# A hybrid decoder layer on one core: the w_ada tiles loaded in one lot, block 2's u summed over six accumulators, the SSM tables queued behind h

## The chip, the core and the metric

The kernel runs on one core of a Trainium2 chip. Its metric is the device time of one execution in microseconds, median of the runs shown. The engines have queues of their own and run side by side: TensorE (PE, with weight loads as PEld), VectorE (DVE), ScalarE (ACT), GpSimd (POOL) and SyncE (SP), which issues nearly all DMAs here.

## The reference, cut to what matters

One decoder layer over 2048 tokens of width 1024. The part in question is the start of the layer:

```python
silu_c = jax.nn.silu(c)
mod = (silu_c @ w_ada[l] + b_ada[l])[:, None, :]
sh_m, sc_m, gt_m, sh_f, sc_f, gt_f = jnp.split(mod, N_MOD, axis=-1)
h = rmsnorm(x, g_mix[l]) * (1.0 + sc_m) + sh_m
proj = h @ w_in[l]
q, k, v, f_logit, u = jnp.split(proj, [...], axis=-1)
...
attn = rmsnorm(forgetting_attention(q, k, v, log_f), g_attn_out[l])
ssm = rmsnorm(s5_ssm(u, a_re[l], a_im[l], log_dt[l], ...), g_ssm_out[l])
mix = jnp.concatenate([attn, ssm], axis=-1) @ w_out[l]
x = x + gt_m * mix
# then a gated MLP with a causal convolution, and a final rmsnorm
```

Nothing of h can be computed before `sh_m` and `sc_m`, the first two sections of silu(c) @ w_ada; and the SSM needs tables that follow from a, dt, B and C alone (powers of exp(lambda dt), sines and cosines).

## The kernel before

Tokens are taken in four blocks of 512 (`TB`), channels in eight tiles of 128 (`KT`), channels on the partitions. All matrix products of the layer are made of three matmuls, hi x hi, hi x lo and lo x hi, of operands split into an fp32r part and its rest: a `w_raw` tile from memory gives `w_hi` on ACT (L86) and `w_lo` on VectorE (L87); a channel tile of h is made by `modulate` as `h_f` (VectorE, L402), `h_hi` (ACT, L390) and `h_lo` (VectorE, L391). There are two `h_f` buffers, and for blocks 2 and 3 each `h_f` is also stored to memory (`f_d`) by SP.

The begin runs like this. `load_x(2)` loads block 2's x and its squares (`sq_acc`, L344), whose sums give the factor `rt` through TensorE, VectorE (`rs_y`), TensorE's transposes (L358) and a copy on ACT (L378). `load_u_weights` loads two weight slots for u. `ada_first` computes the first two sections of the modulation in two halves of 512 channels: 16 tiles `wada` of 256 KB for each half, those of the shift summed by TensorE (L296), those of the scale by VectorE (L298, L300), in 18 buffers that h will use later. The second half's sums end in `mod_gm` and `mod_sm` (L329, L310) of channel tiles 4 to 7. `ssm_tables` then sets up the tables: nine small loads, a chain of some 230 VectorE operations, most of them 128x16, and a function `batches` that makes four batches of larger ones (128x512, 128x576), each with matmuls on TensorE (L787, L788, L802) and stores; batch q may issue after a matmul `marks[q]`.

`proj_u(b)` makes h of a block and projects u and the forget logits: columns in two halves (`cc` 2, 264 wide, and `cc` 3, 256 wide), tokens in four groups `s` of 128. For block 2, half 2 runs k-outer over four accumulators `proj_ps`, so that each channel tile of h is used as it comes; all else is one accumulator after another. An accumulator is copied out by ACT (`f_all` L456, `ust` L458, two buffers) and stored by SP. The order is u of blocks 2, 3, 1, then `proj_qkv(1)`, u of block 0, `proj_qkv(0)`, with three more sections of the modulation (`ada_late`, L319 and L321, w_ada tiles of 512 KB) on VectorE beside them. Attention, SSM, output projection and the MLP follow and are most of the span.

The order in which instructions stand in each engine's queue is set by a scheduler from the program's order, its own estimates, and constraints such as `tc.issue_after(ins)`, which places what is in its block behind the instruction given. Each engine's queue is then worked off strictly in that order.

## Time and profile before

| | |
|---|---|
| median of 3 runs (lowest, highest) | 2625.82 us (2625.49, 2627.09) |
| span of the profiled execution, first to last instruction | 2625.8 us |
| PE, DVE, ACT, POOL busy | 97%, 78%, 48%, 6% |
| mean DMA rate | 197 GB/s |
| span up to block 2's u done / block 1's u done | 83 us / 165 us |

The profiled execution is the one that the page shows; its span agrees with the median, and nothing worth naming lies around it. In the rows of a timeline stand the start and length in us, engine, line, operation, output and inputs; "x4" is a count, and what stands in brackets at the end is the engine's idle time before and what ended it. A bar is longer than the step from one instruction to the next where engines overlap the two.

### The profile page before, as it was taken

What the parts mean: (1) busy time and instruction counts of PE and PEld (TensorE: products, weight loads), DVE (VectorE), ACT (ScalarE), POOL (GpSimd) and SP (SyncE); (2) the same over time, 40 slices, a digit from 0 to 9 for tenths busy, and PEclk for the clock granted to TensorE, in tenths of its full rate; (3) what the DMA queues carried; (4) which work ended last, traced back from release to release, by engine and by line L of the source; (5) the groups of instructions that cost most, each with busy time, mean ns of one, the idle gap of its engine ahead of it and who ended that gap; (6) DMA issues with size and microseconds to landing.
All of it is one profiled execution on the core that took longest, in us unless ns stands there. A gap on an engine that the chain in (4) does not pass through costs nothing.

```text
span 2625.8 us, 35861 instructions
## 1 busy us (share of the span) xinstructions
PE 2539.7 (97%) x12235; PEld 2056.0 (78%) x12235; DVE 2043.4 (78%) x3824; ACT 1257.6 (48%) x2120; POOL 145.9 (6%) x130
## 2 busy tenths in 40 slices
PE   6999999998999999999999999999989999999997
PEld 3888877887788787888778888888767888887776
DVE  7989688966887878787877777776589888876777
ACT  3423255644454545455545555556554555543213
POOL 0001000000000000000000000000002333320000
PEclk8899999998999999999999999999999999999998
DMA  9476986667556655556557555556733443447573
GB/s 318 150 250 217 299 263 199 198 190 236 173 190 215 199 184 184 191 178 207 176 196 224 184 171 192 170 182 225 245 103 128 168 153 136 153 144 289 190 277 119
DMA packets 269319, 516.37 MB, mean 197 GB/s; under 512 B 27952, under 2 KB 114864, under 8 KB 269136
## 3 DMA queue, kind: packets, MB, share of 16 engines
q1 hardware_dynamic: 267312, 508.84, 58.4%
q0 software_dynamic: 1280, 4.20, 0.4%
q8 instruction: 97, 1.59, 0.3%
q10 hardware_dynamic: 544, 1.05, 0.1%
q14 instruction: 86, 0.70, 0.1%
HBM read 374.32 MB, written 139.59 MB: 196 GB/s over the span
## 4 chain that ended last, share of the span: by engine, by line
PE 80%; DMA 7%; DVE 7%; issue 2%; ACT 2%; SPq 1%; POOL 0%; DVEq 0%; POOLq 0%; ACTq 0%
PE ff_ps L1258 19%; PE up_x L1382 7%; PE ff_ps L1232 7%; PE up_z L1382 5%; PE up_y L1382 4%; PE ff_ps L1290 3%; PE ff_ps L1292 3%; PE ff_ps L1291 3%; PE o_ps L1018 2%; PE o_ps L1022 2%; DMA wada<-in_w_ada 2%; PE proj_ps L439 2%; PE acc_x L1612 2%; PE vq_ps L472 2%; PE qs_ps L472 2%
## 5 line engine op out<-in xcount | busy, mean ns | idle before, releaser
L86 ACT CAST w_hi<-w_raw 128x1024 fp32r<-128x1024 f32 (+4 forms) x187 | 173.1, 927 | 270.5 <-DMA w_raw<-in_w_flat 71.6
L1258 PE MATMUL ff_ps<-h_lo,w_hi 128*128 128x512 f32 x704 | 279.8, 397 | 0.8 <-DVE h_lo L391 0.8
L1258 PE MATMUL ff_ps<-h_hi,w_lo 128*128 128x512 f32 x704 | 280.0, 398 | 0.0
L1258 PE MATMUL ff_ps<-h_hi,w_hi 128*128 128x512 f32 x704 | 279.8, 399 | 0.0
L87 DVE TENSOR_TENSOR w_lo<-w_raw,w_hi 128x1024 fp32r<-128x1024 f32 (+4 forms) x187 | 199.8, 1069 | 64.4 <-ACT w_hi L86 52.5
L1009 DVE TENSOR_TENSOR pl<-pf,ph 128x512 fp32r<-128x512 f32 (+1 forms) x320 | 194.9, 618 | 19.8 <-ACT ph L1008 17.1
L1008 ACT CAST ph<-pf 128x512 fp32r<-128x512 f32 (+1 forms) x320 | 177.9, 569 | 62.4 <-PE o_ps L1018 56.4
L1017 DVE TENSOR_TENSOR acc<-acc,pf 128x512 f32<-128x512 f32 (+2 forms) x264 | 159.2, 605 | 26.0 <-ACT pf L1007 23.5
L1007 ACT ACTIVATE pf<-sc_ps 128x512 f32<-128x512 f32 (+2 forms) x184 | 98.3, 539 | 123.3 <-PE sc_ps L998 74.7
L1258 PEld LDWEIGHTS ff_ps<-h_lo,w_hi 128*128 128x128 f32 x704 | 133.6, 190 | 29.5 <-DVE h_lo L391 1.1
L1258 PEld LDWEIGHTS ff_ps<-h_hi,w_lo 128*128 128x128 f32 x704 | 133.5, 190 | 28.8
L1258 PEld LDWEIGHTS ff_ps<-h_hi,w_hi 128*128 128x128 f32 x704 | 133.4, 190 | 28.6 <-issue 0.2
L116 ACT CAST w_hi<-w_raw 128x1024 fp32r<-128x1024 f32 (+2 forms) x100 | 96.4, 964 | 103.7 <-PE ff_ps L1232 41.9
L1291 PE MATMUL ff_ps<-act_lo,w_hi 128*128 128x512 f32 x352 | 139.6, 397 | 0.0
L1290 PE MATMUL ff_ps<-act_hi,w_hi 128*128 128x512 f32 x352 | 139.4, 398 | 0.2 <-ACT rt L378 0.2
L1292 PE MATMUL ff_ps<-act_hi,w_lo 128*128 128x512 f32 x352 | 139.4, 397 | 0.0
L959 DVE TENSOR_REDUCE mx<-sc_ps 128x1 f32<-128x512 f32 (+2 forms) x164 | 97.6, 599 | 52.4 <-PE sc_ps L958 25.9
L1018 PE MATMUL o_ps<-ph,vv 128*128 128x512 f32 (+1 forms) x320 | 121.2, 380 | 2.2 <-ACT ph L1008 2.2
L1022 PE MATMUL o_ps<-pl,vv 128*128 128x512 f32 (+2 forms) x312 | 116.2, 375 | 0.9 <-DVE pl L1009 0.9
L1382 PE MATMUL up_x<-hh,w_hi 128*128 128x512 f32 x352 | 112.7, 400 | 3.4 <-ACT hh L387 1.8
L1364 POOL TENSOR_TENSOR s<-v_raw 128x512 f32<-128x512 f32 x18 | 27.7, 1538 | 1518.9 <-DVE w_lo L87 1518.9
L86 ACT CAST w_hi<-s 128x1024 fp32r<-128x1024 f32 (+2 forms) x66 | 62.1, 944 | 81.8 <-DVE s L1583 31.7
(678 smaller groups left out, 6961.1 us busy)
## 6 DMA issues: line engine op xcount, KB each, us to landing
w_raw<-in_w_flat SPq DMA_DIRECT2D x193, 512.0 KB
w_lo<-wlo SPq DMA_DIRECT2D x68, 512.0 KB
wlo<-w_lo SPq DMA_DIRECT2D x52, 512.0 KB
kb<-kb SPq DMA_DIRECT2D x80, 256.0 KB
vv<-v SPq DMA_DIRECT2D x80, 256.0 KB
w_raw<-in_w_flat SPq DMA_DIRECT2D x40, 384.0 KB
w_raw<-in_w_flat SPq DMA_DIRECT2D x40, 320.0 KB
wada<-in_w_ada SPq DMA_DIRECT2D x48, 256.0 KB
```

The lines of the kernel that those rows point to most:

```text
L86: nc.scalar.copy(hi[:, :n], raw[:, :n])
L87: nc.vector.tensor_tensor(out=lo[:, :n], in0=raw[:, :n], in1=hi[:, :n].bitcast(F32), op=ALU.subtract)
L1008: A.copy(ph[:, cs], pf[:, cs])
L1009: V.tensor_tensor(out=pl[:, cs], in0=pf[:, cs], in1=ph[:, cs].bitcast(F32), op=ALU.subtract)
L1018: T.matmul(o_ps[:, cs], lhsT=vt[:, i, :], rhs=ph[:, cs], start=first, stop=False)
L1022: T.matmul(o_ps[:, cs], lhsT=vt[:, i, :], rhs=pl[:, cs], start=False, stop=(b > 0 and ch == b - 1 and i == 3))
L1232: mark[0] = T.matmul(ps, lhsT=lt, rhs=rt, start=(i == 0), stop=(i == 23))
L1258: T.matmul(ps, lhsT=lt, rhs=rt, start=(n == 0), stop=(n == 23))
L1290: T.matmul(ps, lhsT=a, rhs=ah[:, ts], start=(c == 0), stop=False)
L1291: T.matmul(ps, lhsT=a, rhs=al[:, ts], start=False, stop=False)
L1292: mark[0] = T.matmul(ps, lhsT=bb, rhs=ah[:, ts], start=False, stop=(c == n - 1))
L1382: mark[0] = T.matmul(ps, lhsT=lt, rhs=rt, start=(first and n == 0), stop=(n == 11), skip_group_check=not first)
```

## The change

- `ada_first` has 32 places for its tiles: the 18 h buffers, six `vq` tiles and eight halves of `w_hi`, `w_lo` tiles. No load waits for a tile to come free. The two sums on TensorE share one PSUM tile, in partitions 0 and 32, which leaves the `qs` bank free. The second pair of u weight slots is loaded between the two halves.
- Block 2's u runs k-outer over six accumulators: the four of half 2 and two of half 3, both in the `qs` bank. Two are left for after.
- `ssm_tables` is called after block 2's u and stands behind block 2's last `h_lo`; `proj_qkv(1)` stands behind block 1's last `h_lo`; the four batches stand behind u of block 3, u of block 1, and the first two q tiles of block 1, instead of u of blocks 2, 3, 1 and 1.

```diff
-    def ada_first():
-
-        ps_fns = (vq_ps, lambda: qs_psum.tile([P, TB], F32, name="ada_ps", tag="qs", bufs=1))
+    def ada_first(between):
+
+        places = [hp.tile([P, TB], F32, name="wada", tag=t, bufs=9) for _ in range(9) for t in ("h_hi", "h_lo")]
+        places += [f("wada", [P, TB + 2 * (f is vq_a)], F32)[:, 0:TB] for _ in range(2) for f in (vq_a, vq_b, vq_c)]
+        for tag in ("w_hi", "w_lo"):
+            for _ in range(2):
+                t = wpool.tile([P, 1024], F32, name="wada", tag=tag, bufs=3)
+                places += [t[:, 0:TB], t[:, TB : 2 * TB]]
+        both = vq_ps()
         for hf in range(2):
+            if hf:
+                between()
             cols, js = slice(hf * TB, (hf + 1) * TB), slice(hf * 4, hf * 4 + 4)
             acc = ap_.tile([P, D], F32, name="ada_acc", tag="ada_acc", bufs=2)[:, 0:TB]
-            ps = ps_fns[hf]()
+            ps = both[32 * hf : 32 * hf + 1, :]
             for k in range(KT):
-                wt = [hp.tile([P, TB], F32, name="wada", tag=t, bufs=9) for t in ("h_hi", "h_lo")]
+                wt = [places.pop(0) for _ in range(2)]
                 for sec in range(2):
                     Q.dma_start(wt[sec], w_ada[sec, k, :, cols])
...
+    split_last = [None]
...
-            V.scalar_tensor_tensor(out=lo, in0=f, scalar=shift, in1=hi.bitcast(F32), op0=ALU.add, op1=ALU.subtract)
+            split_last[0] = V.scalar_tensor_tensor(out=lo, in0=f, scalar=shift, in1=hi.bitcast(F32), op0=ALU.add,
+                                                   op1=ALU.subtract)
...
-    def token_rows(pss, h, s0, sl, n):
+    def token_rows(jobs, h):
 
         for k in range(KT):
             hi, lo = h[k]
-            wh, wl = sl[k // 4]
-            c0 = (k % 4) * n
-            for i, ps in enumerate(pss):
-                ts = slice((s0 + i) * P, (s0 + i + 1) * P)
-                lh, ll = hi[:, ts], lo[:, ts]
+            for ps, i, sl, n, first in jobs:
+                wh, wl = (t[:, (k % 4) * n : (k % 4 + 1) * n] for t in sl[k // 4])
+                lh, ll = (t[:, i * P : (i + 1) * P] for t in (hi, lo))
...
     def proj_u(b, rows, wu):
         h = modulate(*rows, mod["gm"], mod["sm"], f_d.get(b))
+        sl = {cc: wu[(cc - 2) * 2 : (cc - 2) * 2 + 2] for cc in (2, 3)}
+        width = {cc: vfu_slots[cc * 2][2] for cc in (2, 3)}
+        done = {}
+        if b == 2:
+            bank = qs_psum.tile([P, TB], F32, name="u_ps", tag="qs", bufs=1)
+            done = {(2, s): (proj_ps(), True) for s in range(4)}
+            done.update({(3, s): (bank[:, s * 256 : (s + 1) * 256], s == 0) for s in range(2)})
+            token_rows([(ps, s, sl[cc], width[cc], first) for (cc, s), (ps, first) in done.items()], h)
         for cc in (2, 3):
-            n = vfu_slots[cc * 2][2]
-            sl = wu[(cc - 2) * 2 : (cc - 2) * 2 + 2]
-            pss = [proj_ps() for _ in range(4)] if (b, cc) in ((2, 2),) else [None] * 4
-            if pss[0] is not None:
-                token_rows(pss, h, 0, sl, n)
-            for s, ps in enumerate(pss):
-                if ps is None:
+            for s in range(4):
+                if (cc, s) in done:
+                    ps = done[cc, s][0]
+                else:
                     ps = proj_ps()
-                    token_rows([ps], h, s, sl, n)
+                    token_rows([(ps, s, sl[cc], width[cc], True)], h)
...
-        ada_first()
-        batches = ssm_tables(pp)
-        wu += load_u_weights(wup, vfu_slots[6:8])
+        ada_first(lambda: wu.extend(load_u_weights(wup, vfu_slots[6:8])))
         marks = []
         for b in (2, 3, 1):
             h = proj_u(b, rows0 if b == 2 else load_x(b), wu)
             marks.append(mark[0])
-        batches(marks + marks[-1:])
+            if b == 2:
+                with tc.issue_after(split_last[0].ins):
+                    batches = ssm_tables(pp)
         rows0 = load_x(0)
-        proj_qkv(1, h, pair_ps(qs_psum))
+        with tc.issue_after(split_last[0].ins):
+            proj_qkv(1, h, pair_ps(qs_psum), marks=marks)
+        batches(marks[1:5])
```

Three places show what the scheduler makes of it. The first is VectorE while block 2's h is made. Before, between the third and fourth of its channel tiles (`ex_`, `sc_` are steps of the tables' chain):

```order
L87 TENSOR_TENSOR w_lo<-w_raw,w_hi 128x1024
L402 SCALAR_TENSOR_TENSOR h_f<-xt,mod_gm,rt 128x512
L87 TENSOR_TENSOR w_lo<-w_raw,w_hi 128x1024
L615 TENSOR_SCALAR sc_sp<-sc_sp 128x16
L620 TENSOR_SCALAR sc_cp<-sc_cp 128x16
L524 TENSOR_SCALAR ex_p<-ex_p 128x16
L402 SCALAR_TENSOR_TENSOR h_f<-xt,mod_gm,rt 128x512
L344 TENSOR_TENSOR sq_acc<-sq_acc,sq 128x512
L614 TENSOR_TENSOR sc_sp<-sc_sp,sc_r_554 128x16
L619 TENSOR_TENSOR sc_cp<-sc_cp,sc_r_554 128x16
L523 TENSOR_TENSOR ex_p<-ex_p,ex_r 128x16
L391 SCALAR_TENSOR_TENSOR h_lo<-h_f,mod_sm,h_hi 128x512
```

Squares, splits and the chain's steps stand between the pieces of h. The same place now, from the second half's `mod_sm` on:

```order
L318 TENSOR_TENSOR mod_sm<-prep_ps,bcol 128x4
L352 TENSOR_TENSOR sq_acc<-sq_acc,sq 128x512 x2
L413 SCALAR_TENSOR_TENSOR h_f<-xt,mod_gm,rt 128x512
L352 TENSOR_TENSOR sq_acc<-sq_acc,sq 128x512
L413 SCALAR_TENSOR_TENSOR h_f<-xt,mod_gm,rt 128x512
L401 SCALAR_TENSOR_TENSOR h_lo<-h_f,mod_sm,h_hi 128x512
L352 TENSOR_TENSOR sq_acc<-sq_acc,sq 128x512 x2
L401 SCALAR_TENSOR_TENSOR h_lo<-h_f,mod_sm,h_hi 128x512
L413 SCALAR_TENSOR_TENSOR h_f<-xt,mod_gm,rt 128x512 x2
L401 SCALAR_TENSOR_TENSOR h_lo<-h_f,mod_sm,h_hi 128x512 x2
```

Only h and the squares of block 3's x are left there; the splits `w_lo` and the chain stand further back. The second place is VectorE behind block 2's last `h_lo`, now:

```order
L401 SCALAR_TENSOR_TENSOR h_lo<-h_f,mod_sm,h_hi 128x512 x2
L675 TENSOR_SCALAR hb<-hb 128x32
L530 TENSOR_SCALAR ex_x<-tb_ld 128x16
L695 MEMSET tb_lr 128x16
L696 MEMSET tb_li 128x16
L712 TENSOR_TENSOR tb_den<-tb_ar 128x16
L713 TENSOR_TENSOR tb_t_891<-tb_ai 128x16
L352 TENSOR_TENSOR sq_acc<-sq_acc,sq 128x512
L531 TENSOR_SCALAR ex_n<-ex_x 128x16
```

There the chain begins, some 100 of its operations ahead of block 3's first `h_f`; before, some 180 stood ahead of that `h_f`, a good half of them ahead of block 2's last `h_lo`. The third place is TensorE at one channel tile of block 2's u, with the buffers' numbers. Before, the tile 882 (`h_hi`) and 883 (`h_lo`) goes through four accumulators, 928 to 931:

```order
L439 MATMUL proj_ps_928<-wu_hi_316,h_hi_882 128x264
L439 MATMUL proj_ps_928<-wu_lo_317,h_hi_882 128x264
L439 MATMUL proj_ps_929<-wu_hi_316,h_hi_882 128x264
L439 MATMUL proj_ps_929<-wu_lo_317,h_hi_882 128x264
L439 MATMUL proj_ps_930<-wu_hi_316,h_hi_882 128x264
L439 MATMUL proj_ps_930<-wu_lo_317,h_hi_882 128x264
L439 MATMUL proj_ps_931<-wu_hi_316,h_hi_882 128x264
L439 MATMUL proj_ps_931<-wu_lo_317,h_hi_882 128x264
L296 MATMUL ada_ps_394<-wada_425,sil_104 1x512
L439 MATMUL proj_ps_928<-wu_hi_316,h_lo_883 128x264
L439 MATMUL proj_ps_929<-wu_hi_316,h_lo_883 128x264
L439 MATMUL proj_ps_930<-wu_hi_316,h_lo_883 128x264
```

After the twelve rows of a tile comes the next tile; half 3 follows when all eight are through. Now the tile 482 and 483 goes through its last rows for four accumulators `proj_ps` and all for one `u_ps`:

```order
L448 MATMUL proj_ps_525<-wu_hi_316,h_hi_482 128x264
L448 MATMUL proj_ps_525<-wu_lo_317,h_hi_482 128x264
L448 MATMUL u_ps_521<-wu_hi_405,h_hi_482 128x256
L448 MATMUL u_ps_521<-wu_lo_406,h_hi_482 128x256
L448 MATMUL proj_ps_522<-wu_hi_316,h_lo_483 128x264
L448 MATMUL proj_ps_523<-wu_hi_316,h_lo_483 128x264
L448 MATMUL proj_ps_524<-wu_hi_316,h_lo_483 128x264
L448 MATMUL proj_ps_525<-wu_hi_316,h_lo_483 128x264
L448 MATMUL u_ps_521<-wu_hi_405,h_lo_483 128x256
L448 MATMUL u_ps_521<-wu_hi_405,h_hi_482 128x256
L448 MATMUL u_ps_521<-wu_lo_406,h_hi_482 128x256
L448 MATMUL u_ps_521<-wu_hi_405,h_lo_483 128x256
```

The rows of `u_ps`, six for each tile, are new: the two accumulators of half 3, token groups 0 and 1, share one bank. Last, ACT between block 2's u and block 3's h, before:

```order
L458 COPY ust<-proj_ps 128x256 x2
L732 COPY tb_lir<-tb_li 128x16 x2
L458 COPY ust<-proj_ps 128x256
L731 COPY tb_lrr<-tb_lr 128x16 x3
L458 COPY ust<-proj_ps 128x256
L732 COPY tb_lir<-tb_li 128x16 x3
L458 COPY ust<-proj_ps 128x256 x2
L378 COPY rt<-misc_ps 128x512
L390 ACTIVATE h_hi<-h_f,mod_sm 128x512 x3
```

and now:

```order
L472 COPY ust<-proj_ps 128x256
L470 COPY f_all<-proj_ps 128x8 x2
L472 COPY ust<-proj_ps 128x256 x2
L472 COPY ust<-u_ps 128x256 x2
L472 COPY ust<-proj_ps 128x256 x2
L386 COPY rt<-misc_ps 128x512
L400 ACTIVATE h_hi<-h_f,mod_sm 128x512 x4
```

The copies to `tb_lrr` and `tb_lir`, part of the chain, are gone from between. In both, all eight copies to `ust` stand ahead of `rt`; before, TensorE's matmuls of half 3 came between them.

More of the change, by code (lines that the diff above doesn't have):

```diff
@@ L282, in vq_c @@
         return vq.tile(shape, dtype, name=name, tag="vq_c")
-    def ada_first():
-        ps_fns = (vq_ps, lambda: qs_psum.tile([P, TB], F32, name="ada_ps", tag="qs", bufs=1))
+    def ada_first(between):
[6 more added lines that the diff above has]
+        both = vq_ps()
         for hf in range(2):
+            if hf:
+                between()
             cols, js = slice(hf * TB, (hf + 1) * TB), slice(hf * 4, hf * 4 + 4)
             acc = ap_.tile([P, D], F32, name="ada_acc", tag="ada_acc", bufs=2)[:, 0:TB]
-            ps = ps_fns[hf]()
+            ps = both[32 * hf : 32 * hf + 1, :]
             for k in range(KT):
-                wt = [hp.tile([P, TB], F32, name="wada", tag=t, bufs=9) for t in ("h_hi", "h_lo")]
+                wt = [places.pop(0) for _ in range(2)]
                 for sec in range(2):
                     Q.dma_start(wt[sec], w_ada[sec, k, :, cols])
-                T.matmul(ps[0:1, :], lhsT=sil[:, k : k + 1], rhs=wt[0], start=(k == 0), stop=(k == KT - 1))
+                T.matmul(ps, lhsT=sil[:, k : k + 1], rhs=wt[0], start=(k == 0), stop=(k == KT - 1))
                 if k == 0:
@@ L305, in ada_first @@
             row = ap_.tile([P, D], F32, name="ada_acc", tag="ada_acc", bufs=2)[:, 0:TB]
-            A.copy(row[0:1, :], ps[0:1, :])
+            A.copy(row[0:1, :], ps)
             pc = prep_ps()
@@ L461, in proj_u, with proj_qkv @@
         return h
-    def proj_qkv(b, h, vq_ps, hook=None, each=iter(())):
+    def proj_qkv(b, h, vq_ps, hook=None, each=iter(()), marks=[]):
         def qk(ms):
@@ L487, in proj_qkv @@
             qk(ms)
+            marks.append(mark[0])
             if ms == (HOOK,) and hook is not None:
```

6 lines of the change are left out of this document (3 added, 3 removed).

## Prediction

> **What bounds the kernel now.** I read the page first, then the busy time by stretches, then TensorE's and VectorE's timelines over 0 to 170 us, the groups on VectorE in the stretch that turned out to matter, and the waits. The page:
>
> ```profile
> span 2625.8 us, 35861 instructions
> PE 2539.7 (97%) x12235; PEld 2056.0 (78%) x12235; DVE 2043.4 (78%) x3824; ACT 1257.6 (48%) x2120; POOL 145.9 (6%) x130
> ```
>
> TensorE is busy for 97% of the span, so 86 us of idle time are all that can be had without taking matmuls out, and this change takes none out. The span of the profiled execution is the median of the runs shown (2625.82) to within 0.1 us; I sum against it. Next, the busy time of each engine by stretch (stretch, its length, busy PE, PEld, DVE, ACT, POOL with counts, granted clock, DMA share, GB/s; the last line sums 345 to 2626 us). I cut where block 2's h is whole (66), its u done (83), block 3's h whole (105.4), its u done and block 1's h begun (119.1), that whole (145.6), block 1's u done (165.3), its qkv done (233), block 0's h whole (251.1):
>
> ```profile
> 0.00:41.40 41.40, 26.96 (x92) 10.38 (x92) 28.05 (x93) 11.98 (x20) 2.96 (x22) 0.96 0.93 328
> 41.40:66.00 24.60, 14.73 (x77) 13.98 (x77) 23.62 (x86) 14.19 (x21) 0.00 (x0) 0.67 0.88 303
> 66.00:83.00 17.00, 15.23 (x113) 15.02 (x113) 16.33 (x87) 5.37 (x28) 0.00 (x0) 0.87 0.25 81
> 83.00:105.40 22.40, 20.50 (x137) 17.85 (x135) 21.18 (x58) 10.96 (x18) 0.00 (x0) 0.85 0.68 218
> 119.10:145.60 26.50, 25.33 (x143) 20.75 (x144) 21.14 (x57) 8.42 (x15) 0.00 (x0) 0.81 0.38 116
> 145.60:165.30 19.70, 19.70 (x141) 18.49 (x141) 17.41 (x44) 5.61 (x15) 0.01 (x1) 1.00 0.84 255
> 165.30:233.00 67.70, 65.31 (x393) 56.49 (x392) 58.00 (x87) 18.27 (x31) 9.54 (x13) 0.97 0.83 275
> 233.00:251.10 18.10, 18.10 (x121) 16.16 (x120) 16.99 (x29) 6.97 (x13) 1.45 (x2) 1.00 0.61 190
> 286.00:347.50 61.50, 57.86 (x363) 51.41 (x363) 36.24 (x60) 17.11 (x30) 1.00 (x2) 0.97 0.96 307
> sum 2281.00, PE 2231.86 PEld 1795.78 DVE 1766.01 ACT 1145.30 POOL 125.82; mean PE 159.42 PEld 128.27 DVE 126.14 ACT 81.81 POOL 8.99
> ```
>
> Three things are seen. The first 41.4 us are DMA: 0.93 of 16 engines at 328 GB/s. From there to 66 us VectorE is the bound: 23.62 of 24.6 us busy, while TensorE issues 77 matmuls. And after 345 us TensorE idles for 49 of 2281 us, so time won ahead of that is kept, unless the order there becomes worse. The events in VectorE's timeline (start us, us):
>
> ```profile
> 43.76 0.15 DVE L310 TENSOR_TENSOR mod_sm<-prep_ps,bcol 128x4 f32<-128x4 f32 x1
> 47.31 0.75 DVE L402 SCALAR_TENSOR_TENSOR h_f<-xt,mod_gm,rt 128x512 f32<-128x512 f32 x1
> 65.04 0.17 DVE L634 TENSOR_TENSOR tb_wc<-sc_t,sc_cp 128x16 f32<-128x16 f32 x1
> 65.12 0.17 DVE L535 TENSOR_TENSOR ex_p<-ex_p,ex_ei 128x16 f32<-128x16 f32 x1
> 65.21 0.75 DVE L391 SCALAR_TENSOR_TENSOR h_lo<-h_f,mod_sm,h_hi 128x512 fp32r<-128x512 f32 x1
> 84.01 1.41 DVE L402 SCALAR_TENSOR_TENSOR h_f<-xt,mod_gm,rt 128x512 f32<-128x512 f32 x2 [0.24 <-ACT rt L378]
> 104.65 0.73 DVE L391 SCALAR_TENSOR_TENSOR h_lo<-h_f,mod_sm,h_hi 128x512 fp32r<-128x512 f32 x1
> 119.15 0.75 DVE L402 SCALAR_TENSOR_TENSOR h_f<-xt,mod_gm,rt 128x512 f32<-128x512 f32 x1 [0.96 <-ACT rt L378]
> 144.84 0.73 DVE L391 SCALAR_TENSOR_TENSOR h_lo<-h_f,mod_sm,h_hi 128x512 fp32r<-128x512 f32 x1
> ```
>
> So block 2's h is whole at 66.0, block 3's takes 84.0 to 105.4, block 1's 119.2 to 145.6. In a row, a 128x16 operation costs 0.08 us (65.04 to 65.12) and an h operation 0.66 (its 0.75 less the overlap). TensorE's side (the number in brackets is its idle time before):
>
> ```profile
> 48.87 0.59 PE L439 MATMUL proj_ps<-wu_hi,h_hi 128*128 128x264 f32 x1 [6.06 <-ACT h_hi L390]
> 60.31 0.42 PE L439 MATMUL proj_ps<-wu_lo,h_hi 128*128 128x264 f32 x1
> 66.64 0.42 PE L439 MATMUL proj_ps<-wu_hi,h_hi 128*128 128x264 f32 x1
> 66.86 0.37 PE L439 MATMUL proj_ps<-wu_lo,h_hi 128*128 128x264 f32 x1
> 67.06 0.28 PE L439 MATMUL proj_ps<-wu_hi,h_hi 128*128 128x264 f32 x1
> 67.18 0.28 PE L439 MATMUL proj_ps<-wu_lo,h_hi 128*128 128x264 f32 x1
> 69.97 0.38 PE L439 MATMUL proj_ps<-wu_hi,h_hi 128*128 128x256 f32 x1 [1.77 <-ACT ust L458]
> 85.56 0.39 PE L439 MATMUL proj_ps<-wu_hi,h_hi 128*128 128x264 f32 x1 [1.90 <-ACT h_hi L390]
> ```
>
> The second half of block 2's u (96 matmuls) starts at 69.97, when all of h has been there for four microseconds, and the next block at 85.56. A matmul's step is 0.12 us at full rate (67.06 to 67.18) and 0.22 at half (66.64 to 66.86).
>
> **The change part by part.** *(a) The w_ada tiles in one lot.* The waits of the second half's loads for free tiles go; nine table loads leave the middle of the SP queue and two 512 KB loads of u weights enter it. The stretch already runs at 328 GB/s; from the bytes alone (1.05 MB in, 0.5 MB out) the last tile comes 1.7 us later, and without the small loads in between somewhat earlier. I take 0, bounds -1 to +2. Ahead of the first h_f stores on SP stand the same loads as before, in another order: 0.
>
> *(b) VectorE before h is whole.* Groups on VectorE, 41.4 to 66 us (count, busy us, mean ns):
>
> ```profile
> L344 DVE TENSOR_TENSOR sq_acc<-sq_acc,sq 128x512 f32<-128x512 f32 x8 | 5.5, 687 | 0.7 <-ACT sq L343 0.7
> L402 DVE SCALAR_TENSOR_TENSOR h_f<-xt,mod_gm,rt 128x512 f32<-128x512 f32 x6 | 4.5, 748 | 0.2 <-DMA f<-h_f 0.2
> L391 DVE SCALAR_TENSOR_TENSOR h_lo<-h_f,mod_sm,h_hi 128x512 fp32r<-128x512 f32 x6 | 4.5, 746 | 0.0
> L87 DVE TENSOR_TENSOR w_lo<-w_raw,w_hi 128x1024 fp32r<-128x1024 f32 x3 | 3.7, 1220 | 0.0
> L87 DVE TENSOR_TENSOR wu_lo<-w_raw,wu_hi 128x1024 fp32r<-128x1024 f32 x2 | 2.4, 1216 | 0.0
> ```
>
> In the new order the two wu_lo stand ahead of the second half's sums, in time that was spent waiting for tiles, and the three w_lo and the table chain behind h. That takes 2.4 + 3.7 us, and for the chain the rest, 23.6 - 20.6 and 2 for the overlap of the 25 long ones, 5: 11 us, so h would be whole at 55. What is late next is the store of h_f: two h_f buffers, each free only when its store has landed, and a store took 5.22 us. The pair after the first two waits besides for block 3's x, whose sums stand ahead of it:
>
> ```profile
> 56.62 5.22 DMA f<-h_f
> ```
>
> ```profile
> 44.20 0.63 ACT L340 ACTIVATE sq_acc<-xt 128x512 f32<-128x512 f32 x1 [1.18 <-DMA xt<-in_x]
> ```
>
> So three pairs of h_f from 45 on, each behind the stores of the one before: 45 + 2 x (0.7 + 5.2) + 1.3 + 1.4 = 59.5 at worst; with stores of 3 us, fewer loads being in the queue, 55. I take 56: 10 us earlier.
>
> *(c) Six accumulators.* With h whole, 2 x 24 matmuls of 128x256 are left instead of 96. At 0.12 us each they cost 5.8; the 18 of the last k another 2.2; and the wait for a copied-out accumulator is 1.8 as at 69.97, or less. Block 2 ends at 56 + 2.2 + 1 + 5.8 = 65 against 83. At half rate the 66 matmuls cost 6.6 more, so 65 to 71. Nothing of TensorE's own work is saved; it is 18 us of waiting that goes. [...]
>
> *(d) What waits for block 2's end.* Block 3's factor rt needs TensorE's transposes, then ACT, whose queue has all eight ust copies ahead of it, with two buffers:
>
> ```profile
> 69.54 0.37 ACT L458 COPY ust<-proj_ps 128x256 f32<-128x256 f32 x1
> 71.98 0.64 ACT L458 COPY ust<-proj_ps 128x256 f32<-128x256 f32 x2
> 159.92 0.71 ACT L458 COPY ust<-proj_ps 128x256 f32<-128x256 f32 x2 [3.72 <-DMA u_d<-ust]
> ```
>
> A pair took 2.4 us where DMA was quiet (69.54 to 71.98), over 4 where it was not. Four pairs from 59: the last copied at 67 to 72. On VectorE some 100 table operations and three sq_acc now stand between the two blocks' h: 100 x 0.08 + 3 x 0.6 = 10 us, to 66. So block 3's first h_f starts at 66 to 72; I take 69, 15 earlier than 84.0. Its h, with what stands between, takes 16 x 0.66 + 5 x 0.6 + 39 x 0.08 = 17 us and some waits, not 21.4: whole at 87. Block 3's u then ends at 87 + 1.4 + 96 x 0.12 = 100 (119), in part because table matmuls have moved behind it. On VectorE 60 rows follow, twelve of them table operations of 512 to 576 columns: 14.5 us, to 101.5. Block 1's h_f starts at 102 (119.2), and its 17 us of rows make h whole at 120 (145.6); block 1's u ends at 120 + 1.4 + 14 x 0.24 + 96 x 0.12 = 136 less what is hidden, 134 (165.3).
>
> *(e) What has been put off.* At that point the new order still owes TensorE 30 qk matmuls of 512 columns at 0.24 us (7.2) and a table batch of 40 small ones (5): 31 - 12 = 19 us ahead. VectorE owes about 24 us of table work (the rows of both orders up to block 1's last h_lo, priced by their form: 118 before, 94 after). Between block 1's and block 0's last h_lo VectorE was busy for 17.41 + 58.00 + 16.99 = 92.4 of 105.5 us; the new order has 101 us there. Of the 13 us it idled, most was this:
>
> ```profile
> DVE ada_acc L321 <- DMA wada<-in_w_ada: 11.7, 6, 3.5
> ```
>
> These waits stay, and the tables' stores come into the same time. 120 + 101 + 12 to 20 = 233 to 241 against 251: 10 to 18 us ahead. The remaining 14 us of tables lie where VectorE is busy for 36 of 61.5 us, and fit. DMA is at 0.96 there; a batch and a half of table stores more (2.5 MB each by the tiles' shapes), at 307 GB/s, are 12 us if nothing hides them and nothing if they go out earlier; I take 2. Later marks for the table batches, and their POOL stores, only fill VectorE and DMA. POOL itself is 6% busy: 0.
>
> Sum, as leads over the old times: 10 at block 2's h, 18 at its u, 15 at block 3's h_f, 17 at block 1's h_f, 26 at its whole h, 31 at its u, of which 12 are TensorE work put off: 19. Of these VectorE and DMA take 3 up to 251 us (inside the 10 to 18 above) and 2 after: -14. **2612 us.**
>
> **The rivals.** *A: all of it is kept.* If VectorE's idle time in 145 to 286 us takes the tables in, the 19 stay and grow a little, since attention also starts with more of block 0's v done: -18 to -25, 2604. For it: TensorE's 97%. Against it: those idle times are waits for DMA, which a compressed begin makes no shorter.
>
> *B: the begin is won, then lost on DMA and VectorE.* From 145 to 233 us DMA has a share of 0.83 to 0.84. If a full 12 us of stores and 3 us of longer waits for w_ada tiles come on top, -14 turns into about 0 to -4: 2624. For it: the share of 0.96 before 347 us. Against: the 0.25 to 0.68 between 66 and 145 us, where the first batch's stores still go.
>
> *C: slower.* The owed table work stands on VectorE, in order, ahead of w_lo and qk_lo of block 1's qkv. If none of its idle time can be used, 24 us of owed work eat the 19; with 12 us of colliding stores it ends 5 to 17 us behind: 2637. It decides when block 1's last h_lo comes later than about 135 us, or VectorE's idle time from there to block 0's h exceeds 35.
>
> *D: the loads decide h.* If the last w_ada tile comes 2 us later and each store takes its 5.2, block 2's h is whole only at 61 and its u at 70; u(3) still starts near 73. Gain 9 instead of 14: 2617, inside my own range.
>
> **How the numbers follow.** Forecast with D 0.63 (2606 to 2620), A 0.13, B 0.14, C 0.10. Faster by over 0.2% (5.3 us, about what a measurement of this kernel tells from no change) means under 2620.6: all of A, nearly all of the forecast: 0.76. B and its edge give 0.14 for the same, C 0.10. The range of 8 in 10 takes in A down to 2599 and B up to 2624; C and B's upper edge are left out. Within the forecast alone it would be 2606 to 2620.
>
> **What would show it.** Right: block 2's last h_lo at 54 to 58, its last u matmul at 65 to 71, block 3's first h_f at 66 to 72, block 1's at 100 to 105, the idle time of TensorE up to 83 us down by some 10 us. ACT's wait for u_d ahead of rt is the new wait. Wrong: h_f waiting for its store over 5 us a pair (D); VectorE's stretch from block 1's h to block 0's longer than 120 us (B, C); TensorE waiting for w_lo or prep_ps in 120 to 250 us; a first attention matmul no earlier than 315 us.

## The result: slower by 0.43%, and the profile after

Five executions of the changed kernel took 2635.03 us in the median (2629.49 to 2640.62), five of the kernel before 2625.49 (2620.80 to 2627.09): ratio 1.0043, 95% interval 1.0028 to 1.0058. The profiled execution, at 2629.49, is the fastest of its five; its page:

```profile
span 2627.8 us, 35809 instructions
PE 2534.9 (96%) x12235; PEld 2051.7 (78%) x12235; DVE 2049.9 (78%) x3824; ACT 1259.1 (48%) x2120; POOL 144.5 (6%) x130
```

Nothing here looks like a loss: TensorE is busy 5 us less, and no engine has changed its share by more than a point. The begin did become faster. VectorE's timeline of the changed kernel:

```profile
58.37 1.41 DVE L401 SCALAR_TENSOR_TENSOR h_lo<-h_f,mod_sm,h_hi 128x512 fp32r<-128x512 f32 x2
72.23 0.75 DVE L413 SCALAR_TENSOR_TENSOR h_f<-xt,mod_gm,rt 128x512 f32<-128x512 f32 x1 [1.13 <-ACT rt L386]
88.45 0.75 DVE L401 SCALAR_TENSOR_TENSOR h_lo<-h_f,mod_sm,h_hi 128x512 fp32r<-128x512 f32 x1
104.26 0.74 DVE L413 SCALAR_TENSOR_TENSOR h_f<-xt,mod_gm,rt 128x512 f32<-128x512 f32 x1
121.42 0.73 DVE L401 SCALAR_TENSOR_TENSOR h_lo<-h_f,mod_sm,h_hi 128x512 fp32r<-128x512 f32 x1
235.59 0.73 DVE L401 SCALAR_TENSOR_TENSOR h_lo<-h_f,mod_sm,h_hi 128x512 fp32r<-128x512 f32 x1
```

Block 2's h is whole at 59.8 (before 66.0), block 3's at 89.2 (105.4), block 1's at 122.2 (145.6), block 0's at 236.3 (251.1). The busy times by stretch, same columns as before:

```profile
0.00:41.40 41.40, 26.95 (x101) 11.55 (x102) 25.75 (x49) 13.21 (x19) 2.97 (x22) 1.00 0.90 321
41.40:66.00 24.60, 18.64 (x144) 18.50 (x144) 19.09 (x64) 15.00 (x31) 0.00 (x0) 0.86 0.76 268
286.00:347.50 61.50, 54.20 (x339) 47.97 (x338) 35.88 (x67) 16.22 (x29) 2.45 (x5) 0.86 1.00 301
345.00:2627.80 2282.80, 2229.47 (x10341) 1793.52 (x10337) 1773.45 (x3070) 1144.43 (x1896) 125.90 (x83) 0.99 0.57 188
```

From 41.4 to 66 us TensorE now issues 144 matmuls in place of 77, and VectorE is no longer the bound (19.09 for 23.62). But from 286 to 347.5 TensorE is busy 54.2 us where it was 57.86, and the granted clock there falls from 0.97 to 0.86.

To see where a lead is lost, I compare work, not events. For an instant of before's trace I take TensorE's work that is still to be done, each matmul priced at the step that its form has there in an unbroken row, and look when the other trace has as much left. The difference is the other kernel's lag in us; negative is ahead:

| kernel | 100 | 300 | 330 | 380 | 540 | 550 | 800 |
|---|---|---|---|---|---|---|---|
| changed | -11.8 | -11.5 | -13.4 | +0.6 | -1.2 | +5.9 | +3.9 |
| e10: begin of before, later order of changed | +3.2 | -2.5 | -7.3 | +6.6 | +4.9 | +12.6 | +7.6 |
| e9: begin of changed, later order of before | -12.2 | -9.5 | -10.9 | +6.9 | +7.4 | +7.3 | +5.3 |
| f8: changed order, short sums | -13.0 | -13.8 | -12.9 | -1.9 | -3.7 | +4.3 | +4.1 |
| f2: changed order, half loads | -12.1 | -13.0 | -16.2 | -3.7 | -5.4 | +3.0 | +4.1 |
| f6: changed order, no third section | -14.1 | -14.2 | -17.5 | -7.0 | -7.9 | +0.2 | -7.7 |
| f1: order of before, half loads | +0.6 | -9.7 | -10.3 | -13.0 | -14.0 | -13.9 | -14.0 |
| f7: order of before, no third section | -0.7 | -8.0 | -8.8 | -12.0 | -12.8 | -12.8 | -12.2 |

The figures are good to about 1 us, since every matmul is priced by its form alone. So the changed kernel is 13.4 us ahead at 330 us, about what was forecast, and loses it at two places: 14.0 us between 330 and 380, and 7.1 more between 540 and 550.

The lead is of another make than forecast. The first 330 us of before and then of the changed kernel:

```profile
0.00:330.00 330.00, 293.21 (x1769) 246.96 (x1770) 267.48 (x741) 104.99 (x209) 20.13 (x47) 0.93 0.76 247
0.00:330.00 330.00, 296.63 (x1863) 251.66 (x1864) 270.66 (x746) 109.81 (x217) 18.64 (x47) 0.96 0.76 247
```

TensorE idles only 3.4 us less (33.4 for 36.8). The rest is rate: the granted clock is 0.96 for 0.93, by an estimate 0.03 x 330 = 10 us of full rate more, and 94 more matmuls have gone through. The first loss is of both kinds too: between 330 and 380 us TensorE idles 13.3 us for 4.5, at a granted clock of 0.80 for 0.91.

The single steps are seen in the windows. First before, 334 to 340 us and 541 to 549 us:

```profile
334.00:340.00 6.00, 5.59 (x37) 4.50 (x37) 4.07 (x9) 3.14 (x7) 0.00 (x0) 1.00 0.96 328
541.00:549.00 8.00, 8.00 (x41) 6.82 (x42) 7.87 (x13) 3.96 (x8) 0.52 (x1) 1.00 0.76 222
```

The same two stretches of the changed kernel:

```profile
334.00:340.00 6.00, 0.33 (x3) 0.28 (x3) 0.75 (x2) 0.65 (x2) 0.00 (x0) 0.61 1.15 324
541.00:549.00 8.00, 3.96 (x24) 2.90 (x22) 7.79 (x15) 6.18 (x12) 0.52 (x1) 0.88 0.18 49
```

In the first, all engines nearly stand still (TensorE 0.33 us busy, VectorE 0.75, ACT 0.65) at a DMA share of 1.15; in the second, VectorE is busy almost throughout (7.79 of 8.00 us) and TensorE half of the time. The changed kernel's waits of TensorE name both, and a third one at the first place (engine, output and line, what it waited for, us, times, longest):

```profile
PE in_ps L855 <- DVE vst L515: 5.7, 1, 5.7
PE sc_ps L1013 <- DMA qa<-rrow: 2.3, 1, 2.3
...
PE qs_ps L486 <- DVE qk_lo L492: 4.8, 1, 4.8
```

**The first place, 330 to 350 us: the cover ended while SP's queue was late.** "Cover" is here work that TensorE can do while something else is awaited. The SSM opens with loads of u (`vin`), and SP issues the first of them only behind the last column sums of the third late section (`prep_ps` from `ada_acc`). The two rows in before:

```profile
305.77 1.48 PE L327 MATMUL prep_ps<-ones,ada_acc 128*128 128x1 f32 x12
309.69 0.60 SPq L915 DMA_DIRECT2D vin<-u_d  x1
```

And in the changed kernel:

```profile
316.28 1.48 PE L335 MATMUL prep_ps<-ones,ada_acc 128*128 128x1 f32 x12
319.20 0.33 SPq L516 DMA_DIRECT2D v<-vst  x1
319.62 0.59 SPq L930 DMA_DIRECT2D vin<-u_d  x1
```

This opening, the "gate" from here on, is 9.9 us later than before, although block 0's h is 15 us earlier: the tables' last VectorE operation moved from 265.1 to 282.7, that of the forget gate stayed (304.7, 302.9), and the third section's sums came last, at 315.8 instead of 304.5. Meanwhile TensorE had used up what it could do. In before, block 0's v projection lies across the opening; two of its six groups, 316 to 350 us (matmuls, busy us, mean ns):

```profile
L439 PE MATMUL vq_ps<-w_hi,h_hi 128*128 128x256 f32 x32 | 9.9, 311 | 3.2 <-DVE qk_lo L478 3.2
L439 PE MATMUL qs_ps<-w_hi,h_hi 128*128 128x256 f32 x24 | 6.9, 289 | 0.3 <-DVE vst L500 0.3
```

The same two groups of the changed kernel:

```profile
L448 PE MATMUL vq_ps<-w_hi,h_hi 128*128 128x256 f32 x16 | 5.1, 319 | 0.0
L448 PE MATMUL qs_ps<-w_hi,h_hi 128*128 128x256 f32 x11 | 3.4, 311 | 0.0
```

Over all six groups 168 matmuls of v were left there in before, the last at 344.9; 83 in the changed kernel, the last at 330.8. The time that TensorE had won had gone into doing this cover earlier.

What it then stood for was not the SSM's data, which ACT began to copy at 326.9. Its first `in_ps` needed an accumulator of v to be copied out to `vst`, and both `vst` buffers still waited to be stored. They were full at 320.6 and 325.8, but on SP their stores stand behind the SSM's loads, which had waited for the gate (SP and ACT, changed kernel):

```profile
332.15 1.92 SPq L516 DMA_DIRECT2D v<-vst  x2
338.84 0.37 ACT L514 CAST vst<-qs_ps 128x256 fp32r<-128x256 f32 x1 [7.82 <-DMA v<-vst]
```

The SSM's first product came 7.9 us earlier (339.7 for 347.6), attention's first score 7.8 us later (323.4 for 315.6).

**The second place, 541 to 549 us: one load ahead of a full VectorE.** The chain of the changed kernel there, in order of time (start us, us, what):

```profile
533.92 6.43 DMA h_f<-f
...
541.13 0.75 DVE h_lo L401
541.88 0.33 DVE m L870
...
548.00 1.14 DVE w_lo L87
549.14 0.61 DVE qk_lo L492
...
549.79 2.50 PE qs_ps L486 x5
```

The reload of h_f took 6.43 us; VectorE has waited 2.0 us for the `h_lo` that needs it, and then works off 8 us of SSM and attention rows before the `qk_lo` that frees TensorE's accumulator. The fourth block's q starts here in both kernels (ACT copies its first q tiles at 541 and 543 in before, at 545 and 548 now), but before's order puts no such wait on TensorE: 8.00 of 8.00 us busy above.

### The profile page after: what moved, and what is told of

It reads as the page before. It is cut to its first block, busy times and chain, and to the rows that moved or that the text cites. A ratio compares the mean times of both kernels' runs of the same rounds, so it can differ in the third digit from the quotient of the medians.

```text
span 2627.8 us, 35809 instructions
## 1 busy us (share of the span) xinstructions
PE 2534.9 (96%) x12235; PEld 2051.7 (78%) x12235; DVE 2049.9 (78%) x3824; ACT 1259.1 (48%) x2120; POOL 144.5 (6%) x130
## 4 chain that ended last, share of the span: by engine, by line
PE 80%; DMA 8%; DVE 7%; ACT 2%; issue 1%; SPq 1%; POOL 0%; POOLq 0%; DVEq 0%; ACTq 0%
PE ff_ps L1275 18%; PE up_x L1399 7%; PE ff_ps L1249 7%; PE up_y L1399 5%; PE up_z L1399 5%; PE ff_ps L1307 3%; PE ff_ps L1309 3%; PE ff_ps L1308 3%; DMA wada<-in_w_ada 3%; PE o_ps L1033 2%; PE o_ps L1037 2%; PE acc_x L1629 2%; PE qs_ps L486 2%; PE vq_ps L486 1%; PE sc_ps L1013 1%
## 5 line engine op out<-in xcount | busy, mean ns | idle before, releaser
L1024 DVE TENSOR_TENSOR pl<-pf,ph 128x512 fp32r<-128x512 f32 (+1 forms) x320 | 195.0, 619 | 26.4 <-ACT ph L1023 25.6
```

The costliest lines, as they stand in the source:

```text
L1024: V.tensor_tensor(out=pl[:, cs], in0=pf[:, cs], in1=ph[:, cs].bitcast(F32), op=ALU.subtract)
```

## The experiments

Each ratio is to the kernel before in the same job, with its 95% interval. "Order held" means that a table in the kernel chains the instructions of each queue, without any semaphore, in the order in which the named kernel ran, so that the edit can't move others; without it the scheduler draws the order anew. No run held an order with nothing else changed, so what the holding itself costs is not measured.

**e1_lot: the w_ada tiles in one lot, alone** (in before).

```diff
+        places = [hp.tile([P, TB], F32, name="wada", tag=t, bufs=9) for _ in range(9) for t in ("h_hi", "h_lo")]
...
+            if hf:
+                between()
```

> The kernel before with the w_ada loads in one lot and the u weights between the halves, nothing else. Two theories. W (wall): the lead of about 12 us that TensorE has until 340 us is lost where attention and SSM begin because the DMA transfers up to there cannot be made earlier; any lead is lost, whichever part makes it. O (order): it is lost because of what this change puts off (tables, block 1's qkv, table batches). Here the table chain still stands ahead of block 2's h, so the lead is small, 2 to 5 us at block 2's u. W: 2623 to 2629. O: 2620 to 2624, the small lead kept.

Measured: 2625.13 us, 1.0004 (0.9991 to 1.0017): no change. Its lag at 330 us is -9.8 and at 800 -2.1.

**e2_lot_six: the same with six accumulators.**

```diff
+            done = {(2, s): (proj_ps(), True) for s in range(4)}
+            done.update({(3, s): (bank[:, s * 256 : (s + 1) * 256], s == 0) for s in range(2)})
```

> The kernel before with the lot and the six accumulators; tables, qkv and batches as before. Both theories: block 2's u ends some 8 us earlier than 83, and a lead of 5 to 8 us at block 1's u (165). W: lost between 340 and 380 us, 2622 to 2630. O: kept, 2616 to 2621.

Measured: 2628.62, 1.0010 (0.9997 to 1.0023): no change.

**e3_tables: the tables behind h, alone.**

```diff
-        batches = ssm_tables(pp)
...
+                with tc.issue_after(split_last[0].ins):
+                    batches = ssm_tables(pp)
```

> The kernel before with the tables' chain behind block 2's last h_lo; loads, accumulators, qkv and batch marks as before. Block 2's h whole at 58 to 62. W: 2622 to 2632, a lead of some 5 us lost like the rest. O: the put-off tables cost and nothing is won for them, 2630 to 2640.

Measured: 2636.33, 1.0045 (1.0031 to 1.0060), as much as the whole change. By itself it makes a lead (-11.7 at 330) and loses it (-0.4 at 380, +11.2 at 800). But its second loss lies elsewhere: nothing goes at 541 to 549 us, and some 14 between 600 and 800. So the move of the tables is enough for a loss of this size; that it is the part that decides in the changed kernel is not shown, for the next run has it as well.

**e4_old_marks: the changed kernel with the batches' old marks, and qkv(1) not held.**

```diff
+        batches(marks + marks[-1:])
-        with tc.issue_after(split_last[0].ins):
-            proj_qkv(1, h, pair_ps(qs_psum), marks=marks)
-        batches(marks[1:5])
+        proj_qkv(1, h, pair_ps(qs_psum))
```

> The changed kernel with the batches behind u of blocks 2, 3, 1, 1 and ahead of block 1's qkv again, and qkv not held behind h. W: the lead at 330 us is lost at the same place, 2626 to 2640. O: the batches' stores go out in the quiet time of DMA before 145 us and the lead stays, 2612 to 2620.

Measured: 2629.55, 1.0015 (1.0003 to 1.0027). About two thirds of the loss go with these constraints, with the tables still behind h. Its trace loses some 12 us at the first place all the same (from -18 at 330 to -6 at 380) and 3 at the second. The parts do not add up, since the scheduler draws the order anew for each.

**e5_before_half and e6_after_half: the three late sections load half of each tile** (the other 512 columns of a section repeat the first; order drawn anew), in before and in the changed kernel.

```diff
-            Q.dma_start(wt, w_ada[sec, k])
+            Q.dma_start(wt[:, 0:TB], w_ada[sec, k, :, 0:TB])
```

> The kernel before with half of the bytes of the late w_ada sections: 24 tiles of 256 KB instead of 512 KB between 165 and 345 us, the loaded half used twice, so VectorE's work stays and the output differs. W (DMA is the wall): some 6.3 MB less, at 307 GB/s 20 us of DMA; before gains little, 0 to 6 us, since its TensorE idles for only 8 us from 165 to 345. V (VectorE is the wall: the equal-work curve of VectorE shows the changed kernel 8 us behind before at 45 to 120 us and level with it from 190 on, while TensorE's shows a lead of 12): 2618 to 2624 too, the waits of ada_acc for wada (some 12 us of VectorE) becoming shorter.

> The changed kernel with the same halved w_ada loads. W: the lead is kept, 2610 to 2616, that is 10 or more us more gained than by the kernel before with the same cut. V: 2620 to 2632, as much gained as before gains, give or take 3 us.

Measured: 1.0049 (1.0034 to 1.0064) and 0.9992 (0.9981 to 1.0003). Less to load made before slower, which the amount of work cannot explain: the order had changed. With the orders held, below, the same edit gives another answer.

**e7_before_short and e8_after_short: some 100 small table operations out** (the exponentials, sines and cosines of the table chain are replaced by short stand-ins).

```diff
-        dtt = exp_acc(pp, ld, sh, "ex1")
+        dtt = ld
```

> The kernel before with some 100 of the tables' small VectorE operations left out (both exponentials and the sine and cosine; constants stand in their place, so the output differs): 8 us of VectorE work less. V: the chain runs there in time that VectorE mostly waits for w_ada tiles, so 2 to 5 us are gained: 2618 to 2623. W and O: nothing, 2622 to 2626.

> The changed kernel with the same 100 operations left out; they stand behind block 2's h, where VectorE has no idle time. V: all 8 us are gained, 2624 to 2629, 4 or more us more than before gains by the same cut. W: nothing, 2632 to 2638, since DMA decides.

Measured: 1.0103 (1.0086 to 1.0120) and 1.0085 (1.0068 to 1.0101). Both lost by doing less; the first lags 23.5 us at 330 already. As a test of VectorE's load the pair decided nothing, and it is why the order was held in the runs below, all but v1.

**e9_after_pinned and e10_before_pinned: the orders exchanged.** Behind block 0's qkv each kernel's queues are held in the order of the other.

```diff
+    n_begin = int(nc.cur_bb.bb.instructions[-1].name.split("-")[1])
...
+    pin_tail(tc, n_begin)
```

> The changed kernel, with every instruction that is written behind block 0's qkv (attention, SSM, MLP: 16,554 of them) held by edges in the same order on each engine as in the kernel before. Theory R (re-drawn order): the change's begin does win 12 us, but the scheduler, which times its own model of the begin, draws another order for attention and SSM, and that order loses them; leaving work out made kernels slower by up to 25 us in the same way. R: the lead is kept, 2610 to 2618. W or V (DMA or VectorE is a wall whatever the order): 2626 to 2636, as the changed kernel.

> The reverse: the kernel before with the changed kernel's order behind block 0's qkv. R: slower than both, 2636 to 2650, since it has the later begin and the worse order. W or V: 2622 to 2630, as before.

Measured: 1.0039 (1.0024 to 1.0054) and 1.0047 (1.0030 to 1.0063). So the later order of the changed kernel costs before's begin 0.47%, with no begin to blame: TensorE's waits in e10, 330 to 600 us, hold both places again; behind the first, ACT stands 9.0 us for the store `v<-vst`.

```profile
PE vq_ps L457 <- DVE vst L518: 8.6, 1, 8.6
PE qs_ps L490 <- DVE qk_lo L496: 4.8, 1, 4.8
```

And before's later order does not fit the new begin either; e9, the same stretch:

```profile
PE qs_ps L504 <- ACT w_hi L86: 10.1, 1, 10.1
PE o_ps L1051 <- DMA vv<-v: 4.0, 1, 4.0
```

TensorE again is 10.9 us ahead at 330 and stands 10.1 us. The row names the weights `w_hi`, but ACT, which makes them, first stood 9.0 us for `v<-vst` and then 3.2 for their load: the first place has the same link as in the changed kernel. The second place is gone (+7.4 at 540, +7.3 at 550).

**f1_before_half_fixed and f2_after_half_fixed: half loads, each kernel's whole order held.** The edit of e5 and

```diff
+    pin_all(tc)
```

> The kernel before with the halved late w_ada loads again, but with the whole order of every queue held as in the kernel before, so that only the bytes differ (the output differs). W1 (bytes of DMA are the wall at 250 to 380 us): some gain, 2612 to 2620. V (VectorE's work is the wall): 2620 to 2626.

> The changed kernel with the halved late w_ada loads and its own order held everywhere. W1: the lead of 12 us stays through 345 to 380 us and the kernel gains 12 to 20 us, 2613 to 2623, at least 5 us more than the kernel before gains by the same bytes. V: 2630 to 2636.

Measured: 0.9984 (0.9970 to 0.9998) and 1.0022 (1.0012 to 1.0032). In before the same edit gives +0.49% with a new order and -0.16% with its own. In f2 the gate opens 3.5 us earlier (first `vin` 316.1), and both losses stay (12.5 and 8.4 us in the table); in f1, whose gate moved from 309.7 to 299.8, neither is there. Its two stretches:

```profile
334.00:340.00 6.00, 6.00 (x41) 5.22 (x40) 5.86 (x10) 5.20 (x10) 0.00 (x0) 1.00 0.91 307
...
541.00:549.00 8.00, 8.00 (x40) 6.54 (x39) 3.86 (x8) 4.49 (x9) 0.00 (x0) 1.00 0.53 162
```

**f3_after_v_pool_fixed: block 0's v stores on GpSimd's queue**, out of the way of SP's loads; order held.

```diff
-                Q.dma_start(v_d[b][s, :, cc * 4 : cc * 4 + 4], vst.bitcast(F32))
+                (G if b == 0 else Q).dma_start(v_d[b][s, :, cc * 4 : cc * 4 + 4], vst.bitcast(F32))
```

> The changed kernel, its order held, with the eight v stores of block 0 on GpSimd's queue instead of behind SSM's loads on SP's. W2 (the order within SP's queue is what holds vst, and so TensorE, for 5.7 us at 334 us): 2624 to 2631. W1 (the DMA engines are full there, whichever queue): 2632 to 2638.

Measured: 2632.07, 1.0042 (1.0026 to 1.0058). The wait of `in_ps` for `vst` is gone, a wait of `sc_ps` for `qa` of 4.9 us stands in its place, and the first `vin` goes at 321.2. SP's queue was only the last link.

**f4_after_pool_fixed: one multiplication of each SSM pair on GpSimd**, order held.

```diff
-            V.tensor_tensor(out=m2, in0=gg, in1=snb, op=ALU.mult)
+            G.tensor_tensor(out=m2, in0=gg, in1=snb, op=ALU.mult)
```

> The changed kernel, its order held, with one of SSM's eight large VectorE multiplications per pair (16 x 0.68 us) on GpSimd, which is idle there. V: 5 to 10 us gained, 2625 to 2630. W1 and W2: the loss at 345 to 380 us stays, 2631 to 2637.

Measured: 2631.20, 1.0037 (1.0023 to 1.0051). From 330 to 600 us GpSimd is busy 26.3 us and VectorE 213.9, for 0.5 and 216.3 in the changed kernel, and the time is the same within the interval; the wait at the second place is 4.4 us for 4.8.

**f6_after_no_tm_fixed and f7_before_no_tm_fixed: without the third late section** (`mod_tm` is set to 1), order held.

```diff
-        ada_late(2, "tm")
+        V.memset(mod["tm"], 1.0)
```

> The changed kernel, its order held, without the third late section of the modulation (8 loads of 512 KB, 8 VectorE operations of 1.28 us, 8 small matmuls; its result replaced by a constant). Theory G (gate): SSM's buffers open only when VectorE has done the last operation of the begin; in the changed kernel that is this section's, at 315.8 us, against 304.5 before, since VectorE works off the tables that were put off first; SSM's first loads follow 4 us later. G: the first load of vin moves from 319.6 to about 307, TensorE's lead of 12 us is kept past 380 us, 2616 to 2624. W1 (bytes): like the halved loads, which took off 6.3 MB and gave 8 us with the lead still lost at 345: 2626 to 2632.

> The same taken out of the kernel before, its order held. G: there forget's last operation ends at 304.7 as well, so the gate hardly moves and only bytes and VectorE time are won: 2614 to 2622, at least 6 us less gained than in the changed kernel. W1: as much gained as in the changed kernel.

Measured: 0.9989 (0.9979 to 0.9999) and 0.9974 (0.9965 to 0.9983). The section's eight tiles, their loads and sums are worth 0.26% to before and 0.54% (0.9989 against 1.0043) to the changed kernel, whose gate then opens at 313.9. That the section stands in the way of the opening is shown, and that it is not all that does; the kernel's two losses of 10.5 and 8.1 us are there nevertheless.

**v1_after_tm_late: that section moved into attention instead**, two steps of `mid` for each place.

```diff
-EACH = 1
+EACH = 2
...
-        ada_late(2, "tm")
-    mid = itertools.chain(*(ada_mid(att_pool, sec, key) for sec, key in ((5, 'tf'),)))
+    mid = itertools.chain(*(ada_mid(att_pool, sec, key) for sec, key in ((2, 'tm'), (5, 'tf'))))
```

> A version to beat both: the changed kernel with that third section moved behind the gate, into the attention stretch, in 256 KB tiles beside the section that is already there (order drawn anew). G: gate near 303 us, lead kept in part, 2612 to 2626. W1 or V: 2628 to 2640, since the same bytes and the same VectorE work come later.

Measured: 2642.76, 1.0074 (1.0049 to 1.0100). It keeps 8.0 us of the lead to 1000 us and then loses 23, to +15.3 at 2000: the order was drawn anew far from the edit.

**f8_after_narrow_fixed: 21 of the late sums only 64 columns wide**, order held, so that VectorE has less to do (23 us by the estimate below; from 286 to 316 us it was busy 12.62 us, in the changed kernel 20.87) and no instruction goes.

```diff
-                E.scalar_tensor_tensor(out=acc, in0=wt, scalar=sil[:, k : k + 1], in1=acc, op0=ALU.mult, op1=ALU.add)
+                E.scalar_tensor_tensor(out=acc[:, 0:64], in0=wt[:, 0:64], scalar=sil[:, k : k + 1], in1=acc[:, 0:64],
+                                       op0=ALU.mult, op1=ALU.add)
```

> The changed kernel with every queue's order held as it ran, in which 21 of the late modulation's VectorE sums (three sections of seven) cover 64 of their 1024 columns; what the other 960 columns should hold is left out. No instruction and no byte of the DMA goes, VectorE loses about 21 x 1.1 = 23 us of the work that the change put off. If VectorE's put-off work is what took the lead away: the last of these sums ends 5 to 12 us earlier (before 315.8), SSM's first load starts with it (before 319.6), TensorE's lead of some 12 us at 330 is still there at 400, and the time is 2612 to 2622. If it is the DMA's bytes before 340 us that took it, the sums end as they did behind their loads, the first product of SSM stays at 339 to 340, and the time is 2630 to 2636.

Measured: 2630.06, 1.0021 (1.0008 to 1.0034). The 12 us that VectorE's amount of work should have given did not come; by the two ratios (1.0043 and 1.0021) about 6 did. VectorE's waits in the changed kernel, 250 to 340 us:

```profile
DVE vst L515 <- ACT vst L514: 10.4, 5, 5.7
DVE w_lo L87 <- ACT w_hi L86: 7.3, 3, 5.1
```

And in f8:

```profile
DVE vst L534 <- ACT vst L533: 13.9, 6, 6.0
DVE w_lo L87 <- ACT w_hi L86: 9.3, 5, 4.0
DVE mod_sf L356 <- PE prep_ps L354: 4.0, 1, 4.0
```

Much of the time freed became waiting: the sums stand in VectorE's queue between v's evictions, which come when TensorE makes them. The last sum ended 2.3 us earlier (313.5), the last column sums stood at their place in TensorE's queue and ended at 318, and the loads followed:

```profile
316.44 1.84 PE L354 MATMUL prep_ps<-ones,ada_acc 128*128 128x1 f32 x16
...
318.32 2.58 SPq L949 DMA_DIRECT2D vin<-u_d  x2
```

## Why the prediction was wrong

The forecast was 2612, the time is 2635, 23 us off. By its own steps:

- *(a) one lot*: 0 was taken; the second half's last `mod_sm` came 0.4 us earlier (43.35 for 43.76). Right.
- *(b) block 2's h whole at 56*: 59.8. The rows that stand there now are short, but `sq_acc` waits for ACT (3.4 us) and the stores do not count (0.3 us). Rival D's 61 was nearer, by another cause.
- *(c) six accumulators, u done at 65 to 71*: the last matmul starts at 69.8. Right in time, but "it is 18 us of waiting that goes" is not what went. Of the 13 us, TensorE's idle time gave 5.7 (20.4 up to 70 us, for 26.1 up to 83), and the same number of matmuls took 7.3 us less of busy time, at a granted clock of 0.95 for 0.86. (So 86 us of idle time were not "all that can be had" either: some 105 us of before's span ran at half clock, by its mean granted clock of 0.980: 0.020 x 2625.8 / 0.5.) The sign named for it, TensorE's idle time up to 83 us down by some 10, came out at 2.4.
- *(d) block 3's first h_f at 69, its h at 87, block 1's at 102 and 120*: 72.2, 89.2, 104.3, 122.2. Each 2 to 3 late, from (b). Right in size.
- *(e) block 0's h at 233 to 241*: 236.3. Right. "The remaining 14 us of tables ... fit" is where it failed: I had compared busy time with idle time in a stretch, and by amount they did fit, for VectorE idles 25.6 of its 61.5 us there in the new trace as well. But the owed work stands ahead of forget and of the third section in VectorE's queue, where its last operation came at 282.7, forget's at 302.9 and the third section's at 315.8, and the last of them opens the SSM. No step priced that place.
- *The sum* took "time won ahead of that is kept, unless the order there becomes worse" from TensorE's 97%. That is the step that failed. The -14 was there at 330 us (-13.4 measured; that it fits so well is in part luck, since most of it is rate and not waiting), and the order behind it did become worse: 14.0 us went between 330 and 380, 7.1 between 540 and 550, and 2 came back by 800. A busy TensorE says that it had work, not that this work could not have served as cover for loads still to come. Before's 168 matmuls of v across the opening were such cover.

Rival C gave 2637, close to the time, and by its mechanism it is wrong: it was to decide if block 1's last `h_lo` came later than 135 us or VectorE idled more than 35 from there to block 0's h; they were 122.2 and 11.9 (102.3 busy in 114.2). The sign that I had named myself did show: attention's first score at 323.4, no earlier than 315.

What the runs show: the later order costs before's begin 0.47% (e10); both losses are there in the changed kernel and in the five runs that hold its whole order (10.5 to 14.0 and 6.1 to 8.4 us; f3 and f4, not in the table, lose 11.1 and 11.4, then 8.4 and 6.1), whether loads, VectorE's work, SP's stores or a whole section are taken out; with before's order held through the whole program, neither is (f1, f7). At the first place the link is the same wherever TensorE stands there and v's stores are on SP: ACT waits 7.1 to 9.0 us for `v<-vst` in the changed kernel, f2, f4, f6, f8, e9 and e10. That is read from the traces. Where the edit took this link out (f3), the wait went to the next; where edits took out load or work ahead of it (f2, f6, f8), 0.21 to 0.54% came back, but not the lead. That the missing cover is the cause is argued from the counts of matmuls (168 and 83); no run gave the cover back alone.

Two things stay open. No order was found that keeps the 13 us: e9 shows that before's later order is not it, and no run beat before without leaving work out. And the traces hold only part of the 9.5 us between the medians. The profiled pair differs by 2.0, at nearly the same granted clock (0.981 and 0.980). Over all five executions of the changed kernel the mean was 0.9786, over the 13 of before that ran beside f8 0.983, and over f8's ten executions the time falls from 2638.19 us at 0.978 to 2621.71 at 0.983. So the rest may go with the clock, but this is not shown, and a lower mean clock is no full account of a loss: e3 and e9 were 0.45% and 0.39% slower at the same mean clock as before beside them (0.983). Why the changed order is granted less was not tried.

## What to carry to other kernels

Before counting a lead as kept, look for the next place where the engine's work needs something from another queue, and ask what will fill the time until it is there: work that is moved ahead is also cover that is taken away. See whether a lead is idle time or rate; a busy share of 97% counts time at half clock as busy (before, 63.0 to 66.6 us: 3.60 of 3.60 us busy at a granted clock of 0.50). Price the put-off work by its place, not by its amount: what stands behind it in the same queue, and which load or buffer that opens. Where a scheduler draws the order, hold the order in the experiments; here the same edit to the same kernel was +0.49% with a new order and -0.16% with the old one.

## What the hardware showed that was not expected

Step (c) left open whether block 2's u would run at half rate or at full rate. In the changed kernel it began at half; TensorE's timeline there:

```profile
48.87 0.59 PE L448 MATMUL proj_ps<-wu_hi,h_hi 128*128 128x264 f32 x1 [5.56 <-ACT h_hi L400]
49.26 0.42 PE L448 MATMUL proj_ps<-wu_lo,h_hi 128*128 128x264 f32 x1
...
52.22 0.28 PE L448 MATMUL u_ps<-wu_hi,h_hi 128*128 128x256 f32 x1
```

After 5.56 us of idling the bars are 0.42 us, and from 52.1 on 0.28: 3.2 us behind the first matmul; the granted clock is 0.50 from 45.24 to 52.07 us and 1.00 from there to 72.55. Before's trace shows longer work at half rate. Two of its windows:

```profile
54.00:60.00 6.00, 2.53 (x16) 2.02 (x16) 6.00 (x16) 3.20 (x5) 0.00 (x0) 1.00 0.87 242
...
63.00:66.60 3.60, 3.60 (x18) 3.60 (x18) 2.91 (x19) 1.77 (x3) 0.00 (x0) 0.50 0.92 345
```

With 2.53 of 6 us busy the granted clock is 1.00; then TensorE works without a gap, and the rate is half from 60.3 to 66.9, 6.6 us. In the records of the granted clock, 17 stretches at half in before and 13 in the changed kernel last 3.4, 6.8, 10.2 or 13.7 us each, without the one at the very end of either trace. At the second place more was lost than the wait: TensorE waited 4.8 us, its next matmuls of 128x512 then came at a step of 0.43 us up to 553.8 and of 0.23 from 554.1 on, and it was 7.1 us behind, with a granted clock of 0.88 from 541 to 549 and of 0.52 from 549 to 554.
